# Values of four heads in one load and results of two heads in one store, in an attention kernel bound by its transfers

## The chip, the cores and the metric

The kernel runs on one core of a Trainium2 chip. The metric is device time in microseconds (us), the median of several executions. Executions of one kernel mostly agree within 0.2%. The time of a run is some 1 to 3 us more than the span that a profile shows from its first to its last instruction, so spans are compared with spans and times with times.

## The reference

```python
# scores [8, 12, 1024, 1024] fp32, v [8, 12, 1024, 64] fp32: 96 heads
attn = np.exp(scores - np.max(scores, axis=-1, keepdims=True))
attn = attn / (np.sum(attn, axis=-1, keepdims=True) + 1e-8)
return np.matmul(attn, v).astype(np.float32)
```

403 MB of scores have to come in. The values and the results are 25 MB each.

## The kernel before

A partition holds eight rows of one head. An iteration of the loop works on four heads (k = 0 to 3); there are 24 iterations. For each row block r of a head, ScalarE takes exponentials to fp16 (two rows at a time), TensorE transposes eight 128x128 blocks into PSUM (psT), VectorE evicts them (pt), and TensorE multiplies by the values. A column of ones beside the values gives the sum of the row. VectorE then normalises (reciprocal and multiplication) and SyncE issues the store.

```python
sc_bh = scores.rearrange("b h (p r) j -> (b h) p r j", p=P)
v_bh = v.rearrange("b h (p c) d -> (b h) p c d", p=P)      # 2 KB runs
out_bh = out.rearrange("b h (p r) d -> (b h) p r d", p=P)  # 2 KB runs
...
    # finish(): after the last row of each half of a head
    if g == G - 1:
        if r == G - 1:
            st["out_sb"] = take(out_bufs)
        recip = take(rc_bufs)
        nc.vector.reciprocal(out=recip[:], in_=psO[:, :, D : D + 1])
        nc.vector.tensor_tensor(
            out=st["out_sb"][:, r - G + 1 : r + 1, :], in0=psO[:, :, 0:D],
            in1=recip[:].to_broadcast([P, G, D]), op=mybir.AluOpType.mult)
    if r == R - 1:
        dma = nc.sync.dma_start(out=one(out_bh, n), in_=st["out_sb"][:])
        ...
def load(k, n, parts=(R,), **cond):
    queue(nc.sync.dma_start(out=v_bufs[k][:], in_=one(v_bh, n), **cond))
    ...                                        # then the scores of the head
def load_next(k, n0):
    if k < AHEAD - 2:                          # heads 0 and 1: within the iteration
        load(k, (n0 + (AHEAD + k)) % BH, cond=n0 < BH - AHEAD)
def load_last(n0):                             # heads 2 and 3: at its end, after the last store
    ...
def heads(n0):
    for k in range(AHEAD):
        nc.gpsimd.tensor_copy(out=vones_bufs[k][:, :, 0:D], in_=v_bufs[k][:])
        ...
```

All transfers go through one queue, in the order in which SyncE issues them. Below, "the third score load" is the load of the next iteration's head 2. It is the first one issued in `load_last`, so it stands behind the last store of the iteration.

The softmax here doesn't subtract the row's maximum and nothing guards it: scores larger than these inputs give would overflow.

Of the kernel before, what the change touches and what calls it, by code (L numbers as in the profile page):

```python
# [14 lines left out]
def kernel(  # L15
# [19 lines left out]
    LAG = 2  # L35
    AHEAD = 4



    sc_bh = scores.rearrange("b h (p r) j -> (b h) p r j", p=P)  # L40
    v_bh = v.rearrange("b h (p c) d -> (b h) p c d", p=P)
    out_bh = out.rearrange("b h (p r) d -> (b h) p r d", p=P)

# [5 lines left out]
    make_identity(nc, ident32)  # L49
    ident16 = const_pool.tile([P, P], FP16, name="ident16")  # L50
    nc.vector.tensor_copy(out=ident16[:], in_=ident32[:])  # L51


    vones_bufs = []
    for k in range(AHEAD):
        vo = const_pool.tile([P, C, M], FP16, name=f"vones{k}")
        nc.vector.memset(vo[:, :, D : D + 1], 1.0)  # L57
        vones_bufs.append(vo)
# [5 lines left out]

    s_bufs = buffers(sb_pool, AHEAD, [P, R, SK], FP32, "s_nat")
    v_bufs = buffers(sb_pool, AHEAD, [P, C, D], FP32, "v_sb")
    p_bufs = buffers(sb_pool, 8, [P, EB, SK], FP16, "p_nat")
    pt_bufs = buffers(sb_pool, 4, [P, SK], FP16, "pt")
    out_bufs = buffers(sb_pool, 4, [P, R, D], FP32, "out_sb")
    rc_bufs = buffers(sb_pool, 4, [P, G, 1], FP32, "recip")  # L70
    psT_bufs = buffers(ps_pool, 4, [P, SK], FP16, "psT")
    psO_bufs = buffers(ps_pool, 4, [P, G, M], FP32, "psO")
    turn = {}
# [20 lines left out]
    def one(bh, n):  # L94
        return bh[bass.ds(n, 1)].rearrange("o p r d -> (o p) r d")

    def finish(u):

        n, r, pt, st = u
        g = r % G  # L100
        if g == 0:
            st["psO"] = take(psO_bufs)
        psO = st["psO"]
        for c in range(C):
            nc.tensor.matmul(  # L105
                out=psO[:, g, :],
                lhsT=pt[:, c * P : (c + 1) * P],
                rhs=st["vones"][:, c, :],
                start=(c == 0),
                stop=(c == C - 1),  # L110
            )
        if g == G - 1:
            if r == G - 1:
                st["out_sb"] = take(out_bufs)
            recip = take(rc_bufs)
            nc.vector.reciprocal(out=recip[:], in_=psO[:, :, D : D + 1])  # L116
            nc.vector.tensor_tensor(  # L117
                out=st["out_sb"][:, r - G + 1 : r + 1, :],
                in0=psO[:, :, 0:D],
                in1=recip[:].to_broadcast([P, G, D]),  # L120
                op=mybir.AluOpType.mult,
            )
        if r == R - 1:
            dma = nc.sync.dma_start(out=one(out_bh, n), in_=st["out_sb"][:])  # L124
            for other in stores:
                apart(dma, other)
                apart(other, dma)
            apart(dma, dma)
            stores.append(dma)
            queue(dma)  # L130
# [8 lines left out]
    def load(k, n, parts=(R,), **cond):  # L139
        queue(nc.sync.dma_start(out=v_bufs[k][:], in_=one(v_bh, n), **cond))  # L140
        r = 0
        for rows in parts:
            queue(
                nc.sync.dma_start(  # L144
                    out=s_bufs[k][:, r : r + rows, :],
                    in_=one(sc_bh, n)[:, r : r + rows, :],
                    **cond,
                )
            )
            r += rows  # L150

    def load_next(k, n0):

# [3 lines left out]
    def load_last(n0):  # L157

        before = queued[-1:]

        def loads(parts2, parts3):
            queued[:] = before
            load(AHEAD - 2, (n0 + (2 * AHEAD - 2)) % BH, parts2)
            load(AHEAD - 1, (n0 + (2 * AHEAD - 1)) % BH, parts3)

        with tc.If(n0 < BH - 2 * AHEAD) as cmp:  # L166
            loads((R,), (R,))
        with cmp.Else():
            with tc.If(n0 < BH - AHEAD):
                loads((4, 4), (2, 2, 2, 2))  # L170

    def heads(n0):

        for k in range(AHEAD):
            nc.gpsimd.tensor_copy(out=vones_bufs[k][:, :, 0:D], in_=v_bufs[k][:])  # L175
            st = dict(vones=vones_bufs[k])
            for r in range(R):
                if r % EB == 0:
                    p_nat = take(p_bufs)
                    rows = 1 if k == AHEAD - 1 and r == R - EB else EB  # L180
                    for g in range(0, EB, rows):
                        nc.scalar.activation(  # L182
                            out=p_nat[:, g : g + rows, :],
                            in_=s_bufs[k][:, r + g : r + g + rows, :],
                            func=EXP,
# [3 lines left out]
                for c in range(C):  # L189
                    nc.tensor.transpose(  # L190
                        out=psT[:, c * P : (c + 1) * P],
                        in_=p_row[:, c, :],
                        identity=ident16[:],
                    )
                pt = take(pt_bufs)
                nc.vector.tensor_copy(out=pt[:], in_=psT[:])  # L196
                if r == R - 1:
                    load_next(k, n0)
                pending.append((n0 + k, r, pt, st))
                if len(pending) > LAG:  # L200
                    finish(pending.pop(0))
        while pending:
            finish(pending.pop(0))
        load_last(n0)

    assert BH % AHEAD == 0 and BH >= 2 * AHEAD
    for k in range(AHEAD):
        load(k, k)
    with tc.For_i(0, BH, AHEAD, iteration_sync="reg_based") as n0:
        queued.clear()  # L210
        heads(n0)
# [30 lines left out]
```

## Time and profile before

| | before |
|---|---|
| time | 1069.1 us (1068.7 to 1069.3) |
| span of the profiled run | 1066.8 us |
| transfers of an iteration | 12 (4 scores, 4 values, 4 stores) |
| period of an iteration, from the completion records | 43.90 us |
| share of the queue's packets in the span | 99.8% |
| last scores landed | 1057.20 us, 9.6 us before the end |

Each transfer leaves 16 completion records, one for each DMA engine. "Landed" means the last of the 16. The period is the mean distance of such completions over 20 iterations, with each transfer's 16 records averaged. This figure, and the others below that come from completion or packet records, are computed from the records in the trace; no view of the profile prints them. How the page reads is told in the prediction, with its lines.

### The profile page before, as it was taken

The numbers are of one execution on the slowest core, as the hardware profiler recorded it, in microseconds if no ns is written. First come the engines' busy times: TensorE is split into PE (matmuls) and PEld (weight loads), VectorE is DVE, ScalarE is ACT, GpSimd is POOL, SyncE is SP. The second block draws the span as 40 slices with busy tenths as digits, with TensorE's granted clock in tenths as the row PEclk, the third lists the DMA queues.
The fourth block names the chain that finished last, engine by engine and source line by source line (L and its number), as shares of the span: only waits on it lengthen the run. The fifth ranks groups of instructions, "written<-read, shape, count | busy, mean of one in ns | idle before, by whom it ended". The sixth has DMA issues, their size and how long they took to land.

```text
span 1066.8 us, 32321 instructions
## 1 busy us (share of the span) xinstructions
PE 762.6 (71%) x12288; PEld 722.4 (68%) x12288; DVE 609.8 (57%) x1157; ACT 736.3 (69%) x432; POOL 59.9 (6%) x102
## 2 busy tenths in 40 slices
PE   3766767677776777668686777767776777767777
PEld 3766766677776767667676767767666677767766
DVE  2655555555564655656565565655555555555556
ACT  4757676676867768577676766677766767667686
POOL 0000000000000000000000000000000000000000
PEclk9888888878888888987888798887898788888889
DMA  9999999999999999999999999999999999999996
GB/s 402 424 425 426 432 431 421 437 434 424 429 430 435 423 440 428 430 429 420 439 430 433 424 432 435 430 423 427 436 433 424 439 422 429 428 439 429 431 423 265
DMA packets 42051, 453.05 MB, mean 425 GB/s; under 512 B 4672, under 2 KB 4672, under 8 KB 29248
## 3 DMA queue, kind: packets, MB, share of 16 engines
q1 hardware_dynamic: 42048, 453.00, 99.8%
q8 instruction: 3, 0.05, 0.0%
HBM read 436.73 MB, written 25.17 MB: 433 GB/s over the span
## 4 chain that ended last, share of the span: by engine, by line
DMA 49%; PE 20%; PEld 9%; ACT 8%; DVE 7%; issue 3%; SPq 3%; DVEq 0%; ACTq 0%
DMA s_nat<-in_scores_dram 49%; PE psT L190 13%; ACT p_nat L182 8%; PE psO L105 7%; PEld L190 6%; DVE pt L196 5%; PEld L105 3%; DVE out_sb L117 2%; SPq L140 1%; SPq L124 1%; SPq L144 1%; DVE recip L116 0%; SPq L166 0%; DVEq L196 0%; ACTq L182 0%
## 5 line engine op out<-in xcount | busy, mean ns | idle before, releaser
L182 ACT ACTIVATE p_nat<-s_nat 128x2048 f16<-128x2048 f32 (+1 forms) x408 | 705.5, 1800 | 253.5 <-DMA s_nat<-in_scores_dram 130.6
L190 PE MATMUL psT<-ident,p_nat 128*128 128x128 f16 x6144 | 583.9, 254 | 257.0 <-ACT p_nat L182 256.1
L196 DVE COPY pt<-psT 128x1024 f16<-128x1024 f16 x768 | 519.2, 690 | 429.2 <-PE L190 138.2
L190 PEld LDWEIGHTS <-p_nat 128*128 128x128 f16 x6144 | 501.3, 154 | 274.9 <-ACT p_nat L182 271.1
L105 PE MATMUL psO<-vones,pt 128*128 128x65 f16 x6144 | 375.8, 205 | 41.8 <-DVE pt L196 37.5
L105 PEld LDWEIGHTS <-pt 128*128 128x128 f16 x6144 | 309.0, 107 | 64.0 <-DVE pt L196 60.3
L175 POOL CAST vones<-v_sb 128x512 f16<-128x512 f32 x96 | 59.2, 617 | 987.7 <-PE L105 443.7
L117 DVE TENSOR_TENSOR out_sb<-psO,recip 128x256 f32<-128x256 f32 x192 | 80.8, 421 | 4.2
L182 ACT ACT_TABLE_LOAD x24 | 30.8, 1283 | 69.6 <-DMA s_nat<-in_scores_dram 64.8
L116 DVE RECIPROCAL recip<-psO 128x4 f32<-128x4 f32 x192 | 33.4, 174 | 18.0 <-PE psO L105 18.0
L57 DVE MEMSET vones<- 128x8 f16 x4 | 0.2, 65 | 0.8 <-PEq L226 0.8
L51 DVE CAST ident<-ident 128x128 f16<-128x128 f32 x1 | 0.2, 228 | 0.3 <-POOL ident masks.py:199 0.3
masks.py:199 POOL TENSOR_SCALAR_AFFINE_SELECT ident<-ident 128x128 f32<-128x128 f32 x1 | 0.3, 293 | 0.1
masks.py:197 POOL MEMSET ident<- 128x128 f32 x1 | 0.2, 204 | 0.3 <-POOLq L226 0.3
L226 POOL MEMSET const-float32-0.0<- 128x1 f32 x1 | 0.1, 98 | 0.2 <-issue 0.2
L226 POOL MEMSET const-bfloat16-1.0<- 128x1 bf16 x1 | 0.1, 101 | 0.0
L226 POOL MEMSET const-uint8-127<- 128x1 uint8 x1 | 0.1, 101 | 0.0
L226 POOL MEMSET const-float32-1.0<- 128x1 f32 x1 | 0.1, 98 | 0.0
## 6 DMA issues: line engine op xcount, KB each, us to landing
s_nat<-in_scores_dram SPq DMA_DIRECT2D x96, 4096.0 KB, 27.1
v_sb<-in_v_dram SPq DMA_DIRECT2D x98, 256.0 KB, 20.6
out_dram<-out_sb SPq DMA_DIRECT2D x96, 256.0 KB, 18.0
s_nat<-in_scores_dram SPq DMA_DIRECT2D x2, 2048.0 KB, 19.9
s_nat<-in_scores_dram SPq DMA_DIRECT2D x4, 1024.0 KB, 18.7
```

The source lines that it names most:

```text
L51: nc.vector.tensor_copy(out=ident16[:], in_=ident32[:])
L105: nc.tensor.matmul(out=psO[:, g, :], lhsT=pt[:, c * P : (c + 1) * P], rhs=st["vones"][:, c, :], start=(c == 0), stop=(c == C - 1),)
L116: nc.vector.reciprocal(out=recip[:], in_=psO[:, :, D : D + 1])
L117: nc.vector.tensor_tensor(out=st["out_sb"][:, r - G + 1 : r + 1, :], in0=psO[:, :, 0:D], in1=recip[:].to_broadcast([P, G, D]), op=mybir.Al ...
L124: dma = nc.sync.dma_start(out=one(out_bh, n), in_=st["out_sb"][:])
L140: queue(nc.sync.dma_start(out=v_bufs[k][:], in_=one(v_bh, n), **cond))
L144: nc.sync.dma_start(out=s_bufs[k][:, r : r + rows, :], in_=one(sc_bh, n)[:, r : r + rows, :], **cond,)
L175: nc.gpsimd.tensor_copy(out=vones_bufs[k][:, :, 0:D], in_=v_bufs[k][:])
L182: nc.scalar.activation(out=p_nat[:, g : g + rows, :], in_=s_bufs[k][:, r + g : r + g + rows, :], func=EXP,)
L190: nc.tensor.transpose(out=psT[:, c * P : (c + 1) * P], in_=p_row[:, c, :], identity=ident16[:],)
L196: nc.vector.tensor_copy(out=pt[:], in_=psT[:])
L226: nc = _bacc.Bacc("TRN2", target_bir_lowering=False, num_devices=1)
```

## The change

The intent is to use fewer and longer DMA runs for the same bytes. One load brings the values of four heads in runs of 8 KB, 32 partitions per head. One store takes the results of two heads in runs of 4 KB, 64 partitions per head. To put rows and columns where this needs them, the exponentials are written in another order and the transposes use a permuted identity. Each result tile is filled by multiplications of 64 partitions. The values are cast at once on GpSimd and then spread over all partitions by 16 copies on VectorE.

```diff
-    v_bh = v.rearrange("b h (p c) d -> (b h) p c d", p=P)
-    out_bh = out.rearrange("b h (p r) d -> (b h) p r d", p=P)
+    v_bh = v.rearrange("b h (i t) d -> (b h i) (t d)", i=Q)
+    out_bh = out.rearrange("b h (j x) d -> (b h j) (x d)", j=W)
...
-    psO_bufs = buffers(ps_pool, 4, [P, G, M], FP32, "psO")
+    psO_bufs = buffers(ps_pool, 2, [P, R // G, 512], FP32, "psO")
...
+    def normalise(k, st, first, last):
+        ...
+        nc.vector.reciprocal(out=recip, in_=psO[:, :, :, D : D + 1])
+        h = k % T
+        for t in range(T):
+            part = slice(t * W, (t + 1) * W)
+            rows = st["out_sb"][h * W : (h + 1) * W, t, first * G : last * G, :]
+            nc.vector.tensor_tensor(...)        # 64 partitions
...
+        if k == AHEAD - 1:
+            if g == G - 1:
+                normalise(k, st, b, b + 1)      # head 3 in two halves
+        elif r == R - 1:
+            normalise(k, st, 0, R // G)         # heads 0 to 2 whole
+        if r == R - 1 and k % T == T - 1:       # one store for two heads
+            dma = nc.sync.dma_start(...)
...
+    def spread_v(k):
+        for s in range(S):
+            nc.vector.tensor_copy(
+                out=vones_bufs[k][s * Q : (s + 1) * Q, :, 0:D],
+                in_=v_half[k * Q : (k + 1) * Q, s],
+            )
...
         with tc.If(n0 < BH - 2 * AHEAD) as cmp:
             queued[:] = before
-            load(AHEAD - 2, (n0 + (2 * AHEAD - 2)) % BH, parts2)
-            load(AHEAD - 1, (n0 + (2 * AHEAD - 1)) % BH, parts3)
+            load(AHEAD - 2, (n0 + (2 * AHEAD - 2)) % BH)
+            load_v((n0 + 2 * AHEAD) % BH)
+            load(AHEAD - 1, (n0 + (2 * AHEAD - 1)) % BH)
...
-                loads((4, 4), (2, 2, 2, 2))
+                load(AHEAD - 2, BH - 2, (4, 4))
+                load(AHEAD - 1, BH - 1, (2, 2, 2, 1, 1))
```

## The prediction

> **What bounds the kernel now.** I read the page's engine totals first, then the DMA rows of its slices, then the queue table and the transfer list.
>
> ```profile
> PE 762.6 (71%) x12288; PEld 722.4 (68%) x12288; DVE 609.8 (57%) x1157; ACT 736.3 (69%) x432; POOL 59.9 (6%) x102
> DMA  9999999999999999999999999999999999999996
> GB/s 402 424 425 426 432 431 421 437 434 424 429 430 435 423 440 428 430 429 420 439 430 433 424 432 435 430 423 427 436 433 424 439 422 429 428 439 429 431 423 265
> q1 hardware_dynamic: 42048, 453.00, 99.8%
> s_nat<-in_scores_dram SPq DMA_DIRECT2D x96, 4096.0 KB, 27.1
> v_sb<-in_v_dram SPq DMA_DIRECT2D x98, 256.0 KB, 20.6
> out_dram<-out_sb SPq DMA_DIRECT2D x96, 256.0 KB, 18.0
> ```
>
> No compute engine is over 71%, while the 16 DMA engines are full in every slice but the last. A score load takes 27.1 us to land because others are queued ahead of it. The transfers are the bound, so only two things can shorten the run: fewer DMA microseconds for the same 453 MB, or a shorter stretch after the last score has landed. The waits and the end of the chain show that stretch:
>
> ```profile
> ACT p_nat L182 <- DMA s_nat<-in_scores_dram: 130.6, 28, 7.5
> SPq L124 <- DVE out_sb L117: 234.5, 50, 9.0
> ...
> 1055.84 0.69 DVE pt L196
> 1057.40 1.06 ACT p_nat L182
> 1060.27 0.64 DVE pt L196
> 1060.96 0.67 PE psO L105 x8
> 1061.65 0.19 DVE recip L116
> 1061.87 0.42 DVE out_sb L117
> ```
>
> In the body ScalarE waits for scores. At the end the last piece of scores lands at 1057.20 us (the completion records), and the exponential of its rows starts at 1057.40, a start that had waited for TensorE as well. So there the data and the compute arrive together, 9.6 us before the end of the span at 1066.8. Work added to the compute of the last heads is therefore not free.
>
> **What the Trainium skill says.** "DMA: Bandwidth & Descriptors", section "Why small descriptors are slow (HBM only)", gives each packet a fixed overhead of about 3 cycles beside its bytes. The trace agrees in kind: 2 KB packets last a median 84 ns, 8 KB ones 309, 32 KB ones 1213, which is 9 ns plus the bytes at 27.2 B/ns. The same page, "Anatomy of one DMA", puts about 2 us of fixed cost on one DMA. That does not apply to a full queue here: a 256 KB transfer lands 0.63 to 0.68 us after the one in front. "ScalarE: Activation LUTs", section "What ACT_TABLE_LOAD costs", gives 186 ns + 0.833 ns per element, so 1892 ns for 2048; the trace has 1901. "VectorE: DVE Perf Modes", section "Side-by-side: where the cycles go for N=2048 bf16", gives about 150 cycles plus the elements of one partition over the mode's rate of 1, 2 or 4 a cycle; the trace's eviction of 1024 fp16 values from PSUM (690 ns) and its multiplication of 256 fp32 values (421 ns) fit that at two and one elements a cycle of 0.96 GHz.
>
> **The DMA part, which is the aim.** Bytes don't change; counts do. An iteration of four heads issues 12 transfers now (4 scores, 4 values, 4 stores) and 7 after (4, 1, 2). There are two ways to price the difference, and they disagree.
>
> By packet durations: 12,288 value packets of 84.5 ns become 3,072 of 310; 12,288 store packets become 6,144 of some 160 (interpolated); some 1,900 completion packets of 9 ns go. That is 84.7 + 56.3 + 17.1 = 158 us over 16 engines, 9.9 us of the run.
>
> By landings: packets overlap a little (the DMA share in the windows is 1.01), so what counts is the interval between completions in a full queue. Averaged over 21 iterations a score load adds 9.68 us, a value load 0.634, a store 0.662; four of each make 43.90, which is the measured period. In the last iteration the score load is cut in pieces, so the sizes of interest are there: a 1 MB load of 8 KB runs adds 2.453, a 2 MB one 4.86. These points lie on a line of 2.407 us per MB plus 0.046 per transfer. So the new value load, just such a 1 MB transfer of 8 KB runs, costs 2.45 in place of 4 x 0.634 = 2.54, and two stores of 512 KB (by the line 1.25, and 0.02 more behind a load, as now) 2.53 in place of 2.65. The period falls by 0.09 + 0.12 = 0.21 us, to 43.69; over 24 iterations **5.0 us**. I choose this one: it prices exactly what the next transfer waits for.
>
> Does the queue stay full? In DMA time from the landing of an iteration's first score load: second score load lands at 9.7, stores at 12.2, third score load begins there. It is issued after the store of heads 2 and 3. Head 3 landed at -9.7, its compute takes some 12 us, so the issue comes near 3, about 9 us early. The out tiles fall from four to two double ones; the store of heads 0 and 1 lands near 11 to 12, and the multiplication that reuses its tile stands behind the third eviction of the next head, near 15. So neither wait bites.
>
> **The compute part.** VectorE loses nothing and gains two things. Values: the four casts an iteration on GpSimd (617 ns each) become one wide cast there and 4 x 4 copies on VectorE of 32x512 fp16, SBUF to SBUF, a quarter cycle per element: (150+128)/0.96 = 290 ns at most, perhaps 200; 384 of them make 80 to 110 us. The built order puts all 16 ahead of the iteration's first eviction, so one block of some 4 to 5 us. Normalisation: half the partitions in each instruction saves no time, so for three heads of four 0.18 + 2 x 0.69 = 1.56 us (now 2 x (0.17+0.42) = 1.19), and for the fourth 2 x (0.17 + 2 x 0.42) = 2.03. Over 24 iterations 24 x (3 x 0.37 + 0.84) = 47 us. VectorE comes to about 610 + 95 + 47 = 752 us, some 71%: on a par with TensorE, and under the transfers.
> GpSimd: 24 casts of 2048 columns at some 2.4 us by the 617 ns for 512; off the path. ScalarE: same elements, read as runs of 8 floats with gaps; I take 1.90 as now. TensorE: same counts.
> In the body all this hides: a head needs some 8.5 us in a burst (1036.5 to 1062 for three), the transfers give it 10.9. Even with the copies ahead of it, head 0 is caught up by head 2.
>
> **The end.** It hangs on the landing of head 93's scores, 1034.5 now, the last one that found TensorE idle. By then 94 value loads and 89 stores have landed (94 x 0.634 = 59.6 us of DMA time and 89 x 0.662 = 58.9); after, 24 value loads of 2.453 and 44 stores of 1.265: 58.9 and 55.7. So that landing comes 4.0 us earlier. From there the transfers need two stores, 2 x 4.86 for head 94, then three pieces of 1 MB and two of 0.5 MB for head 95: 22.1 us (now 22.75), and the last row then some 5 us to the end of its multiplication: 27.1 from that landing. By compute, three heads took 27.85 us from it (1034.45 to 1062.3); the block of copies adds about 1 (four transposed rows wait in PSUM meanwhile), the longer normalisation 0.4 to 0.8 a head, mostly hidden: 29 to 29.5. The last store of 0.5 MB lands 0.6 us later than one of 256 KB. If compute sets the end: -4.0 + 1.4 + 0.6 = -2.0, 1067.2. If data does: -4.0 - 0.75 + 0.6 = -4.15, 1065.0. I can't tell which and take the middle: **1066 us**, 0.3% faster.
>
> **Rivals.** First, the packet durations are right and the saving is 9.9 us, of which the end gives back some: 1060 to 1062. For it: the packet sum accounts for 99.8% of the span. Against it: landings of 1 MB and of 256 KB transfers side by side. Second, ScalarE becomes the bound: if the runs of 32 bytes slow the exponential, 1.90 would have to grow over 2.7 us before its 7.6 us a head pass 10.9; a growth of 10% would show only at the end, 2 to 3 us: 1068 to 1071. The 154 ns for weight loads from the strided p_nat against 107 from pt show that strides can cost; those are 2-byte elements apart by 16 bytes, here 32 bytes are together. Third, VectorE's copies wait on each other (each waits for the one before it), take 0.4 us each and, with TensorE held up, the queue still holds 9 us: no change in the body, 1 to 3 us at the end: 1068 to 1070. Fourth, a store that waits on two heads delays a load: against it the 9 us above; it would cost up to 24 times a few us, 1090 and more.
>
> **Range and chances.** The two ends give 1065.0 and 1067.2. Below them lies the full 5.0 us with an end 1 us shorter, 1063, and the packet rival, near 1061. Upwards the end can take 3 us more (second and third rivals). I give 1061 to 1070. A change of 2% is 21 us; no saving of DMA time allows it, and slower by that needs the second or fourth rival in full.
>
> **What would show it.** Right: q1's share stays at 99% or more with 24,900 packets in place of 42,048; the value load lands 2.45 us behind its predecessor, the store pair 1.25 to 1.28; the period is 43.7; VectorE about 750 us busy; the end from the last landing 9 to 12 us. Wrong: a period of 43.5 or less (the packet rival), slices with DMA under 9 (starvation), an exponential over 2.0 us, copies over 0.35 us.

## The result

The changed kernel takes 1075.1 us (1074.75 to 1075.75, four runs). The kernel before, on the same chip, takes 1069.1. The ratio is 1.0057, with a 95% interval of 1.004 to 1.0075. So the change is 0.6% slower, which is within 2% but outside the predicted range of 1061 to 1070. Ratios here are the mean time of one kernel's fast runs over that of the other's from the same rounds, so they are not quite the ratio of the quoted medians.

The page of the changed kernel, with the rows that answer to those of the prediction (engine totals, DMA row of the slices, queue table, transfer list):

```profile
PE 737.2 (69%) x12288; PEld 700.7 (65%) x12288; DVE 775.5 (72%) x1517; ACT 736.0 (69%) x432; POOL 48.1 (4%) x31
DMA  9999999999999999999999999999999999999993
q1 hardware_dynamic: 24912, 453.00, 98.8%
s_nat<-in_scores_dram SPq DMA_DIRECT2D x96, 4096.0 KB, 24.7
v_sb<-in_v_dram SPq DMA_DIRECT2D x24, 1024.0 KB, 18.2
out_dram<-out_sb SPq DMA_DIRECT2D x48, 512.0 KB, 10.6
```

The counts are as planned: 24,912 packets and seven transfers an iteration. VectorE has grown by 166 us. The DMA row looks as full as before. The 10.6 us of the stores is a median over two kinds: by the completion records, the store of heads 0 and 1 lands 26.1 us after its issue and that of heads 2 and 3 only 7.7 us, where an iteration's last store took 11.9 us before. So less work stands in the queue when the last store is issued, and this turns out to matter.

The groups of VectorE that are new (busy time, then mean ns of one), from the same page:

```profile
L120 DVE TENSOR_TENSOR out_sb<-psO,recip 64x512 f32<-64x512 f32 (+1 forms) x240 | 139.7, 582 | 7.7
L195 DVE COPY vones<-v_half 32x512 f16<-32x512 f16 x384 | 109.4, 285 | 23.2 <-POOL v_half L190 6.0
```

The waits of the changed kernel (us in total, times, longest):

```profile
ACT p_nat L230 <- DMA s_nat<-in_scores_dram: 228.7, 49, 5.9
PE psO L135 <- DVE out_sb L120: 39.1, 24, 1.8
...
SPq L149 <- DVE out_sb L120: 694.8, 47, 20.0
```

ScalarE waits longer for scores than before (228.7 against 130.6 us). TensorE has a new wait of 1.6 us in each iteration: the multiplications of rows 4 to 7 of head 3 wait for the normalisation of rows 0 to 3, because both halves are now one PSUM tile. The store holds SyncE for 694.8 us in all, where it was 234.5.

**Two differences in time.** The last scores land at 1057.09 us (before: 1057.20), so the transfers gained nothing. From there to the end of the span it takes 16.4 us (before: 9.6). The chain that ends last shows this stretch; with the last scores in at 1057.1, VectorE still has rows of the last head to evict seven microseconds later:

```profile
1064.11 0.68 DVE pt L248
...
1065.74 2.06 PE psO L135 x32
...
1067.83 0.19 DVE recip L115
...
1068.55 0.38 DVE out_sb L120
```

**Where the late end comes from.** This is VectorE's timeline at the start of the last iteration of the changed kernel (start, length, instruction, in brackets the idle time before it and what ended that):

```profile
1028.01 0.18 DVE L115 RECIPROCAL recip<-psO 128x4 f32<-128x4 f32 x1 [1.42 <-PE psO L135]
1028.23 0.88 DVE L120 TENSOR_TENSOR out_sb<-psO,recip 64x256 f32<-64x256 f32 x2
1029.69 5.04 DVE L195 COPY vones<-v_half 32x512 f16<-32x512 f16 x16 [0.58 <-PE psT L242]
1034.75 1.89 DVE L248 COPY pt<-psT 128x1024 f16<-128x1024 f16 x3
```

And the same place in the kernel before:

```profile
1024.03 0.42 DVE L117 TENSOR_TENSOR out_sb<-psO,recip 128x256 f32<-128x256 f32 x1
1027.89 0.69 DVE L196 COPY pt<-psT 128x1024 f16<-128x1024 f16 x1 [3.43 <-PE L190]
```

Before, VectorE is done with the old iteration 0.9 us after the first scores of the new one have come in (ScalarE's table load at 1023.54 marks that), and then idles 3.4 us until exponentials and transposes arrive. After, it is done 4.3 us after that mark (1024.81), and then the block of 16 copies takes 5.0 us more. So the first eviction stands 9.9 us behind the mark, where it stood 4.35. From the first eviction to the end of the last multiplication the four heads then take 34.2 us (before 34.4). The sum closes: first scores 1.27 us later, first eviction 5.59 us later from there, 0.23 us less for the four heads and 0.11 us more for the last store make 6.74 us, and the spans differ by 1073.51 - 1066.77 = 6.74.

**Where the transfers lost their gain.** The period of an iteration is 43.89 us, as before (43.90); 43.69 was predicted. Yet each kind of transfer costs what was predicted when one lands behind another: the value load 2.450 us, the store 1.261, a score load a median of 9.690. What is new is packets that last too long. If a packet counts as long when it lasts over 25 ns more than 9.2 ns plus its bytes at 27.2 B/ns, the kernel before has 15 such packets after the first 75 us (in which all kernels show some) and the changed one 263. Their excess, summed and divided by 16 engines, is 4.55 us (before 0.04). That is the missing saving. They lie 3 to 10 us behind the landing of an iteration's first scores, which is where SyncE issues the last store and the third score load.

### The profile page after: what moved, and what is told of

It reads as the page before. It is cut to its first block, busy times and chain, and to the rows that moved or that the text cites. A ratio compares the mean times of both kernels' runs of the same rounds, so it can differ in the third digit from the quotient of the medians.

```text
span 1073.5 us, 32452 instructions
## 1 busy us (share of the span) xinstructions
PE 737.2 (69%) x12288; PEld 700.7 (65%) x12288; DVE 775.5 (72%) x1517; ACT 736.0 (69%) x432; POOL 48.1 (4%) x31
## 3 DMA queue, kind: packets, MB, share of 16 engines
q1 hardware_dynamic: 24912, 453.00, 98.8%
## 4 chain that ended last, share of the span: by engine, by line
DMA 60%; PE 18%; ACT 7%; DVE 5%; issue 3%; SPq 3%; PEld 3%; DVEq 0%; ACTq 0%; PEldq 0%
DMA s_nat<-in_scores_dram 60%; PE psT L242 11%; ACT p_nat L230 7%; PE psO L135 7%; DVE out_sb L120 2%; DVE pt L248 2%; PEld L242 2%; SPq L183 1%; SPq L171 1%; PEld L135 1%; SPq L149 1%; DVE vones L195 0%; DVE recip L115 0%; SPq L209 0%; ACTq L230 0%
## 5 line engine op out<-in xcount | busy, mean ns | idle before, releaser
L230 ACT ACTIVATE p_nat<-s_nat 128x2048 f16<-128x2048 f32 (+1 forms) x408 | 705.2, 1800 | 260.1 <-DMA s_nat<-in_scores_dram 228.7
L242 PE MATMUL psT<-order,p_nat 128*128 128x128 f16 x6144 | 582.5, 249 | 141.8 <-ACT p_nat L230 137.2
L248 DVE COPY pt<-psT 128x1024 f16<-128x1024 f16 x768 | 511.4, 689 | 227.2 <-PE psO L135 94.3
L242 PEld LDWEIGHTS <-p_nat 128*128 128x128 f16 x6144 | 490.3, 153 | 152.7 <-ACT p_nat L230 150.6
L135 PE MATMUL psO<-vones,pt 128*128 128x65 f16 x6144 | 355.2, 205 | 187.9 <-DVE pt L248 147.8
L135 PEld LDWEIGHTS <-pt 128*128 128x128 f16 x6144 | 297.1, 106 | 213.4 <-DVE pt L248 166.3
L120 DVE TENSOR_TENSOR out_sb<-psO,recip 64x512 f32<-64x512 f32 (+1 forms) x240 | 139.7, 582 | 7.7
L195 DVE COPY vones<-v_half 32x512 f16<-32x512 f16 x384 | 109.4, 285 | 23.2 <-POOL v_half L190 6.0
L190 POOL CAST v_half<-v_sb 128x2048 f16<-128x2048 f32 x25 | 47.4, 1897 | 1000.6 <-DMA v_sb<-in_v_dram 704.4
L115 DVE RECIPROCAL recip<-psO 128x8 f32<-128x8 f32 (+1 forms) x120 | 22.8, 190 | 34.0 <-PE psO L135 19.8
## 6 DMA issues: line engine op xcount, KB each, us to landing
out_dram<-out_sb SPq DMA_DIRECT2D x48, 512.0 KB, 10.6
```

The costliest lines, as they stand in the source:

```text
L115: nc.vector.reciprocal(out=recip, in_=psO[:, :, :, D : D + 1])
L120: nc.vector.tensor_tensor(out=rows.rearrange("j (b g) d -> j b g d", g=G), in0=psO[part, :, :, 0:D], in1=recip[part].to_broadcast([W, last ...
L135: nc.tensor.matmul(out=st["psO"][:, b, g * M : (g + 1) * M], lhsT=pt[:, c * P : (c + 1) * P], rhs=st["vones"][:, c, 0:M], start=(c == 0), ...
L190: nc.gpsimd.tensor_copy(out=v_half[:], in_=v_sb[:])
L195: nc.vector.tensor_copy(out=vones_bufs[k][s * Q : (s + 1) * Q, :, 0:D], in_=v_half[k * Q : (k + 1) * Q, s],)
L230: nc.scalar.activation(out=p_nat[:, g : g + rows, :].rearrange("p r (s v) -> p s r v", s=S), in_=s_bufs[k][:, r + g : r + g + rows, :].rea ...
```

## The experiments

Three theories for the transfers were tried, one after the other. **P**: a burst of issues that falls late into the load in flight disturbs them, whatever made it late. **B**: large transfers straight behind each other do, above all the first two score loads, which have nothing between them any more. **Q**: the third score load is issued too late, behind the two-head store, so that the faster DMA engines run nearly out of work. For the end there was one theory (the copies and the late normalisation add up) and, as rivals, that one of the two alone does it. The texts are quoted as they stood before each run, with letters of their own: A is the block of 16 copies as the cause of both losses, C the normalisation on 64 partitions and the two-head stores, D the common PSUM tile, F an early form of P, and L (in store_pad and values_pad) the shared completion semaphores. All results were correct, but for one run that is named.

### First four: each half of the change alone, the copies elsewhere, the copies alone

store_only keeps the store part and takes the values back to the code of before. values_only is the reverse.

```diff
# store_only, against the changed kernel
+        queue(nc.sync.dma_start(out=v_bufs[k][:], in_=one(v_bh, n), **cond))
...
-            spread_v(k)
+            nc.gpsimd.tensor_copy(out=vones_bufs[k][:, :, 0:D], in_=v_bufs[k][:])
# values_only, against the changed kernel
-        if r == R - 1 and k % T == T - 1:
+        if r == R - 1:
+            dma = nc.sync.dma_start(out=one(out_bh, n), in_=st["out_sb"][:])
```

> Only the stores are changed (two heads in one 512 KB store, permuted transposes, half-partition normalisation); values as before. Theory A (the 16 value copies on VectorE, in one 5.0 us block at the start of each iteration, cause both losses): no block, so the stream gains its 2.9 us (24 x 0.12), the end grows by at most 1 to 1.5 us from the longer normalisation and the larger last store; 1066.5 to 1068.5 us, score packets over 1233 ns as few as before (65). Rival C (the normalisation on 64 partitions and the stores of two heads hold the compute up): 1072 or more. Rival B (score loads queued back to back lengthen the packets): value loads still stand between them, so few long packets.

> Only the values are changed (one 1 MB load for four heads, cast, 16 copies, permuted exponential); stores and normalisation as before. Theory A: the whole loss is here: end from the last landing some 15 us as in the changed kernel (9.6 before), and the stream loses 4 to 5 us by some 250 long packets while it gains 2.0: 1074 to 1076 us. Rival C: the loss is not here: 1067 to 1069. Rival B: the long packets stay, since loads stand back to back except for small stores, and the end is short: 1069 to 1071.

Measured: store_only 1162.2 us (ratio 1.0868, interval 1.085 to 1.0886), values_only 1153.9 us (1.0789, 1.0771 to 1.0807). Both are far slower than either whole kernel, and neither was foreseen. The waits of SyncE say why, first of store_only, then of values_only:

```profile
SPq L167 <- DMA v_sb<-in_v_dram: 218.0, 22, 10.5
SPq L171 <- DMA s_nat<-in_scores_dram: 201.1, 23, 8.9
```

```profile
SPq L156 <- DMA s_nat<-in_scores_dram: 487.0, 25, 21.9
```

SyncE waits, before it issues a load, for another load to land. The completion records show the reason: an iteration's transfers take eight completion semaphores in turn, and the turn begins anew with each iteration. A semaphore is not taken again before its last transfer has landed. With 12 transfers (before) or seven (after) this falls on transfers that have long landed, or are soon to. With nine, the ninth and the next iteration's first share a semaphore and stand side by side in the queue; with ten it is two pairs. These two runs therefore measure the number of transfers, not the parts of the change; the same two parts with 12 transfers, in the second four, take 1084.2 and 1072.5 us.

spread_pool moves the copies to GpSimd. before_copies adds 16 such copies, of no use, to the kernel before, at the same place.

```diff
# spread_pool, against the changed kernel
-            nc.vector.tensor_copy(
+            nc.gpsimd.tensor_copy(
                 out=vones_bufs[k][s * Q : (s + 1) * Q, :, 0:D],
# before_copies, against the kernel before
+        for k in range(AHEAD):
+            for q in range(4):
+                nc.vector.tensor_copy(
+                    out=idle_b[k][q * 32 : (q + 1) * 32, :, 0:D],
+                    in_=idle_a[k * 32 : (k + 1) * 32, q],
+                )
```

> The changed kernel with the 16 copies moved from VectorE to GpSimd; transfers the same. Theory A: the block is gone; the end from the last landing falls from 16.4 to 10 to 11.5 us; if the copies also caused the long packets, the last score lands near 1052.5 in place of 1057.1: 1063 to 1066 us. If the long packets come from loads queued back to back (rival B) they stay: end short, landing near 1057: 1068 to 1070. Rival C: 1073 or more.

> The kernel before with 16 idle copies of the same shape and the same quarters of partitions on VectorE at the start of each iteration, into tiles that nobody reads; transfers the same. Theory A: end from the last landing from 9.6 to 14 to 15 us (1073 to 1074), and if the copies themselves lengthen packets, the last landing 4 to 5 us later (1077 to 1079). Rival B: long packets don't come, so 1073 to 1074. Rival C: nothing much, 1069 to 1071.

Measured: spread_pool 1071.7 us (1.0026, 1.0009 to 1.0043), before_copies 1068.7 us (1.000, 0.9983 to 1.0016). Taking the copies off VectorE brings the end from 16.4 to 12.1 us behind the last landing. The landing itself stays (1057.5 us), and so do the long packets (4.39 us). So the copies cost some 4 us at the end and nothing in the stream. In the kernel before, the same block costs nothing at all:

```profile
1024.01 0.42 DVE L120 TENSOR_TENSOR out_sb<-psO,recip 128x256 f32<-128x256 f32 x1
1025.35 5.06 DVE L179 COPY idle_b<-idle_a 32x512 f16<-32x512 f16 x16 [0.91 <-DVE out_sb L120]
1030.44 1.89 DVE L205 COPY pt<-psT 128x1024 f16<-128x1024 f16 x3
```

The block begins in the 3.4 us in which VectorE idled, delays the first eviction by 2.5 us, and the four heads catch up on these, since they waited for data (31.9 us instead of 34.4). In the changed kernel the old iteration ends late, and the block then stands behind it.

### Second four: the parts again with 12 transfers, head 3 in one piece, another order

store_pad and values_pad are the two halves with tiny loads of 512 bytes added (two and three in an iteration), so that the count is 12 again. values_pad also issues the value load ahead of the third score load. no_split normalises head 3 whole, as the other heads. order_v puts the value load behind the first score load.

```diff
# store_pad, against store_only (values_pad is alike, with three)
+    def pad(j):
+        rows = v.rearrange("b h s d -> (b h s) d")
+        queue(nc.sync.dma_start(out=pad_bufs[j][:], in_=rows[0:16, 0:8]))
# no_split, against the changed kernel
-        if k == AHEAD - 1:
-            if g == G - 1:
-                normalise(k, st, b, b + 1)
-        elif r == R - 1:
+        if r == R - 1:
             normalise(k, st, 0, R // G)
# order_v, against the changed kernel
+            if k == 0:
+                load_v((n0 + 2 * AHEAD) % BH, cond=n0 < BH - 2 * AHEAD)
...
-            load_v((n0 + 2 * AHEAD) % BH)
```

> The stores alone changed, as in the first store run, with two tiny loads of 16 rows of 32 bytes an iteration so that twelve transfers share the eight completion semaphores exactly as before. Theory L (the 1162 us of the store run came from its ten transfers: loads waited for the landing of a load issued just before on the same semaphore): the queue is full again and the time falls to 1066 to 1070. If it stays over 1100, theory L is wrong. Theory D (rows 4 to 7 of an iteration's last head wait for the multiplication of rows 0 to 3, since both banks are one tile): about 2 us more at the end than before, so nearer 1068 to 1070; end from the last landing 11.5 to 12.5.

> The values alone changed, with three tiny loads an iteration for the same purpose. Theory L: full queue. The stream gains 2 us at most and keeps the long packets away if they come from score loads standing back to back (here a store stands between them): last landing near 1055, end some 9.6 us later: 1067 to 1069, for the 5 us block of copies cost nothing in the kernel before. If the long packets come with the one large value load or the permuted exponential, last landing near 1059 and 1071 to 1072.

> The changed kernel with the last head normalised whole, like the other three, in place of in halves. Theory D: the stall of TensorE before the last 32 matmuls of each iteration (39 us in all, 1.6 to 1.8 each) is gone, the multiplications after the last matmul grow from 0.9 to 1.4 us, so each iteration's compute ends 1.5 to 2 us earlier; the end from the last landing falls from 16.4 to 13 to 14.5 us: 1071.5 to 1073.5. If the stall is no cause: 1075 to 1076.

> The changed kernel with the value load issued after the first score load of the next iteration in place of between the last two, so that no three score loads stand back to back. Rival B (back to back loads lengthen packets): the 4.5 us of long packets fall under 1 us and the last landing comes at 1052 to 1054, the end follows as far as compute allows: 1071 to 1073. Rival F (the burst of issues right behind the last store of an iteration lengthens the packets in flight): three issues remain of four, long packets fall by a third at most: 1074 to 1075.

Measured: store_pad 1084.2 us (1.0142, 1.0125 to 1.0159), values_pad 1072.5 us (1.0031, 1.0014 to 1.0048), no_split 1074.0 us (1.0046, 1.0029 to 1.0063). Two numbers carry weight. First, values_pad has almost no long packets (0.05 us) and a period of 43.81: the value part saves the 0.09 us that were predicted for it. store_pad has 1.70 us of long packets and no saving (43.92). So the loss in the stream comes with the store. Second, the old iteration's last multiplication ends 1.3 us behind the mark of the new one before, 1.4 in values_pad, 3.5 in store_pad, 4.6 in the changed kernel (means over 21 iterations). So the store part makes the end late and the value part puts its copies behind it. The times of the two carry less. In store_pad's last iteration the multiplication waits once for a cast that had waited for a score load on a shared semaphore:

```profile
PE psO L139 <- POOL vones L210: 12.2, 1, 12.2
```

Without that it would be near 1072 us (an estimate: 1084.2 less 12.2). In values_pad, head 94's first exponential starts only when the second half of its scores has landed, some 5 us late. no_split shortens the delay by 0.7 us. Its time is 1.1 us lower, but the intervals of the two ratios overlap, and it misses the 1071.5 to 1073.5 us of its theory: the wait on the common PSUM tile is real but small.

order_v gave a wrong result (relative error 1.36): the value load overtook the cast of the values it replaces. Its time says nothing.

### Third four: theories P and Q, and the late end without its causes

before_late holds back the last reciprocal of each iteration of the kernel before by 14 copies (4.7 us). order_v2 is order_v repaired. banks_pool is the changed kernel with the copies on GpSimd and one PSUM tile per half head, so that neither cause of the late end is left. banks_pool_early is banks_pool with the third score load issued ahead of the iteration's last store.

```diff
# before_late, against the kernel before
+            if k == AHEAD - 1 and r == R - 1:
+                for q in range(14):
+                    after(nc.vector.tensor_copy(...))   # ahead of the reciprocal
# banks_pool, against the changed kernel
-    psO_bufs = buffers(ps_pool, 2, [P, R // G, 512], FP32, "psO")
+    psO_bufs = buffers(ps_pool, 4, [P, G, M], FP32, "psO")
...
-            nc.vector.tensor_copy(
+            nc.gpsimd.tensor_copy(
# banks_pool_early, against banks_pool
+        elif k == AHEAD - 2:
+            load(k, (n0 + (AHEAD + k)) % BH, cond=n0 < BH - 2 * AHEAD)
...
-            load(AHEAD - 2, (n0 + (2 * AHEAD - 2)) % BH)
```

> The kernel before with 14 idle copies on VectorE (4.4 us) between the last eviction of each iteration and its last reciprocal, so that the last multiplication, the last store and the burst of loads behind it come some 3.4 us later, as in the changed kernel (4.6 us behind the landing of the next head in place of 1.3). The end is 3.4 us later in any case: 1072.5. Theory P (long packets come where the burst of issues falls that late into the load in flight, whatever made it late): 3 to 5 us of long packets, last landing 1060 to 1062: 1075.5 to 1077.5. If not P: last landing 1057.

> The changed kernel with the copies on GpSimd and with one PSUM tile per bank, every head normalised by halves as before. Theory D: no stall of TensorE before the last 32 matmuls; the last multiplication 2 us nearer to the landing of the next head (4.6 to about 2.5); the end from the last landing 10 to 10.5 us (12.1 with the copies moved alone). Theory P: long packets fall from 4.4 to 1 to 2 us, last landing 1054 to 1055: 1066 to 1068. If P is wrong but D right: 1069 to 1070.

> As banks_pool, with the third score load of the next iteration issued before the last store, so that it isn't held by that store and only the store, the value load and the fourth score load stand in the burst. Theory P: long packets under 1 us, last landing 1052.5 to 1054, 1064 to 1066. If the long packets have nothing to do with the burst: as banks_pool.

> The changed kernel with the value load issued right behind the first score load of the next iteration, this time with the cast ahead of it in the program (the first try cast the values of the wrong iteration). Rival B (three score loads back to back): long packets under 1 us, last landing 1052 to 1054, 1070 to 1073. Theory P: the burst is as late as before, with three loads less one: 3 to 4.5 us of long packets stay, 1074 to 1076.

Measured: before_late 1072.9 us (1.0041, 1.0025 to 1.0058), banks_pool 1070.4 us (1.0013, 0.9996 to 1.0029), banks_pool_early 1071.0 us (1.0018, 1.0001 to 1.0034), order_v2 1088.6 us (1.0185, 1.0166 to 1.0204).

- **P fell.** In before_late the old iteration's last multiplication ends 5.3 us behind the mark of the new one, later than in the changed kernel (4.6). It pays 3.7 us for this at the end (13.3 us behind the last landing instead of 9.6), but has only 0.24 us of long packets.
- **The late end is explained for the most part.** In banks_pool the end is 11.95 us behind the last landing, within the 9 to 12 of the prediction (its own expectation, 10 to 10.5, missed), at a nearly unchanged landing of 1056.9 us. Of the 2.4 us that are left over the kernel before, 1.8 come from the landing, which follows the first scores of the last iteration sooner: after 31.9 us there, after 33.7 before. VectorE's timeline shows the block gone:

```profile
1028.40 0.88 DVE L119 TENSOR_TENSOR out_sb<-psO,recip 64x256 f32<-64x256 f32 x2
1029.75 1.29 DVE L246 COPY pt<-psT 128x1024 f16<-128x1024 f16 x2 [0.47 <-PE L240]
```

- **Q gained.** banks_pool_early moves nothing but the third score load. Its long packets fall from 4.03 to 0.90 us (0.65 of it in the last iteration) and its period to 43.69 us, although its old iterations end 6.3 us behind the mark (banks_pool: 3.9), which speaks against P once more. The time did not follow, for two reasons of this build. In the last iteration its second store comes when most engines have no work left: the issue ends at 1031.57 us, and the fastest engine was done at 1028.57. And its exponentials of head 2 wait on a semaphore shared with the value load:

```profile
ACT p_nat L229 <- DMA v_sb<-in_v_dram: 160.0, 22, 7.4
```

- **B lost.** order_v2 has the value load between the first two score loads, where the long packets lie, and more of them (11.66 us), not fewer. Its value load also has to wait for the cast of the values before it, so the run is not a clean one.

### Fourth: the third load moved, and the converse

after_early is the changed kernel with the third score load moved ahead of the last store. Two more things change with it, though its text says one: the value load now stands behind the fourth score load, and head 94's scores come as one piece where they came in two halves. (The clean move is banks_pool_early, above.) before_later is before_late with 24 copies instead of 14. banks_pool_early2 is banks_pool with the move of after_early.

```diff
# after_early, against the changed kernel
-        if k < AHEAD - 2:
+        if k < AHEAD - 1:
             load(k, (n0 + (AHEAD + k)) % BH, cond=n0 < BH - AHEAD)
...
-            load(AHEAD - 2, (n0 + (2 * AHEAD - 2)) % BH)
-            load_v((n0 + 2 * AHEAD) % BH)
             load(AHEAD - 1, (n0 + (2 * AHEAD - 1)) % BH)
+            load_v((n0 + 2 * AHEAD) % BH)
...
-                load(AHEAD - 2, BH - 2, (4, 4))
# before_later, against before_late
-                for q in range(14):
+                for q in range(24):
```

> The changed kernel with one thing moved: the third score load of an iteration is queued ahead of its last store (after head 2's exponentials) instead of behind it. Theory Q (the load held behind the two-head store runs the queue of the fastest DMA engines nearly dry): long packets in the body fall from 4.55 us to below 1 us, the last scores land at 1053 to 1054.5 us instead of 1057.1, and the time falls to 1069 to 1072 us, since the late end (16 us after the landing) is untouched. Rival (the long packets come from the large transfers themselves, wherever the load is issued): long packets stay at 4 us or more, landing at 1057, time 1075 us.

> The kernel before with 24 idle copies (about 7 us) ahead of the last reciprocal of an iteration, which holds its last store and so the third score load back some 7 us. Theory Q: the fastest DMA engines run nearly dry, so the body shows 3 us or more of long packets, the last scores land at 1060 us or later, and the time is 1078 to 1081 us. Rival (lateness of the load has nothing to do with it, the large transfers have): long packets below 0.5 us, last landing 1057 to 1058 us, time 1075.5 to 1077 us from the later end alone.

> Both repairs together: copies on GpSimd and one PSUM tile per bank (no late end), and the third score load ahead of the last store, this time with the exponentials' semaphore not shared with the value load. If the two causes are the whole of it: last scores land at 1053 to 1054.5 us, the end comes 10 to 12.5 us later, 1064 to 1067 us, which is what was predicted for the change. If the gain in the stream is given back in a third place: 1069 us or more.

Measured: after_early 1069.5 us (1.0008, 0.9993 to 1.0024), before_later 1109.9 us (1.0377, 1.0361 to 1.0393), banks_pool_early2 1069.3 us (1.0007, 0.9994 to 1.0021).

after_early's edit takes the ratio from 1.0057 to 1.0008, some 5 us. Its long packets fall from 4.55 to 0.14 us and its period to 43.68 us; the last scores land at 1052.31 us instead of 1057.09. The queue's side can be read from SyncE's timeline, here the last store of an iteration and the third score load. In the kernel before around 542 us:

```profile
541.94 0.33 SPq L124 DMA_DIRECT2D out_dram<-out_sb  x1
543.41 0.35 SPq L144 DMA_DIRECT2D s_nat<-in_scores_dram  x1
```

When this load's issue ended (543.76), the fastest engine had 7.4 us of work left (until 551.17). In the changed kernel around 547 us:

```profile
546.96 0.35 SPq L149 DMA_DIRECT2D out_dram<-out_sb  x1
547.85 0.35 SPq L171 DMA_DIRECT2D s_nat<-in_scores_dram  x1
```

By the completion records of that iteration, the first scores landed at 542.14 us. The work queued ahead of these two issues, the second score load and the store of heads 0 and 1, was completed at 549.36 us on the fastest of the 16 engines and at 553.07 on the slowest. So the fastest engine had 2.1 us of work left when the store was issued (its issue ended at 547.31), and 2.4 us, with the new store, when the score load was. In after_early:

```profile
567.08 0.36 SPq L149 DMA_DIRECT2D out_dram<-out_sb  x1
568.40 0.34 SPq L171 DMA_DIRECT2D s_nat<-in_scores_dram  x1
```

Here the load is issued at the end of head 2's exponentials, 23 us before the work ahead of it is done on the fastest engine (591.98 us). The mean over the engines doesn't tell this: that engines finish a transfer independently is stated by the Trainium skill, "DMA: Bandwidth & Descriptors", section "Why a DMA increments its semaphore by 16 and not by 1". The traces agree: the first and the last of the 16 completions of a large transfer lie 2.3 to 3.1 us apart before and 2.7 to 4.1 after. So I call **lead** the time from the end of an issue to the completion, on the fastest engine, of the transfer ahead of it. The smallest lead of all issues of an iteration, as a mean over 20 iterations, beside the long packets:

| kernel | smallest lead, us | long packets, us | period, us |
|---|---|---|---|
| before_later | 1.2 | 25.07 | 45.41 |
| order_v2 | 1.8 | 11.66 | 44.32 |
| spread_pool | 2.5 | 4.39 | 43.89 |
| changed kernel | 2.5 | 4.55 | 43.89 |
| banks_pool | 2.8 | 4.03 | 43.87 |
| no_split | 3.1 | 3.79 | 43.86 |
| before_late | 3.5 | 0.24 | 43.90 |
| store_pad | 4.3 | 1.70 | 43.92 |
| values_pad | 6.4 | 0.05 | 43.81 |
| before_copies | 7.5 | 0.04 | 43.90 |
| before | 7.6 | 0.04 | 43.90 |
| banks_pool_early | 8.3 | 0.90 | 43.69 |
| after_early | 15.2 | 0.14 | 43.68 |
| banks_pool_early2 | 15.6 | 0.26 | 43.68 |

The order is not perfect: store_pad stands out (its single leads go down to 2.8 us), and banks_pool_early does by its last iteration alone. But the two pairs that move only the time of issue, banks_pool to banks_pool_early and before_late to before_later, move the long packets in both directions. And B falls: after_early and banks_pool_early have the same large transfers, the first two score loads still back to back, and few long packets. The converse went much further than expected: before_later was to take 1078 to 1081 us under Q and took 1109.9. With a lead of 1.2 us the fastest engines run dry: by the packet records, fewer than 16 packets are in flight for 45.9 us between 75 and 1000 us, a mean of some 2 us an iteration (before: none; changed kernel: 1.7 us in all). And a late load makes the next heads late as well. The packets' share of the span tells the two costs apart:

```profile
q1 hardware_dynamic: 42048, 453.00, 98.4%
```

98.4% of 1109.1 us is 1091.4 us of packet time, 26.7 more than before (99.8% of 1066.8), nearly all of it long packets. The other 15.6 us of the longer span are time without packets, 8.1 of them at the end (17.7 us from the last landing instead of 9.6).

The end of after_early was expected and stays late, 14.5 us behind the last landing. That of banks_pool_early2 was not: 14.6 us, with neither copies nor a common tile in its way. ScalarE's timeline of that kernel shows a wait that the edit itself had brought:

```profile
1030.72 7.32 ACT L226 ACTIVATE p_nat<-s_nat 128x2048 f16<-128x2048 f32 x4 [1.06 <-DMA s_nat<-in_scores_dram]
1041.84 14.63 ACT L226 ACTIVATE p_nat<-s_nat 128x2048 f16<-128x2048 f32 x9 [3.80 <-DMA s_nat<-in_scores_dram]
```

Head 94's scores, now one piece, land at 1041.7 us. ScalarE idles 3.8 us for them, and then the exponentials of two heads fill the rest.

### Last two: both repairs

after_early3 and banks_pool_early3 bring head 2's scores in two halves again, in every iteration (eight transfers).

```diff
# both, against after_early and banks_pool_early2
+            parts = (4, 4) if k == AHEAD - 2 else (R,)
-            load(k, (n0 + (AHEAD + k)) % BH, cond=n0 < BH - AHEAD)
+            load(k, (n0 + (AHEAD + k)) % BH, parts, cond=n0 < BH - AHEAD)
```

> after_early with the load of head 2 of each iteration in two halves, so that head 94's first half lands some 5 us before its second, as in the kernels before and changed (in after_early it is one piece, and the exponentials of the last two heads, 14.6 us of them, all wait for its landing at 1041.3 us). If the whole piece is what held the end of after_early: the last exponential starts at about 1052.5 instead of 1055 us, the span falls by 1 to 2.5 us, and the time is 1067 to 1068.5 us, limited then by the copies at the start of the last iteration (34 us of work from their end). Rival (the end is set by the matmul and copy chain alone): 1069 to 1070 us as in after_early.

> The same edit on banks_pool_early2, which has neither the copies on VectorE nor the split stall. Last scores land at 1052.5 to 1053 us as there; the last exponential starts at 1053 instead of 1055.4 us, the span ends 10 to 12 us after the landing: 1064 to 1066 us, faster than the kernel before by 0.3 to 0.45%. Rival (something other than the whole piece held the end): 1069 us again.

Measured: after_early3 1069.9 us (1.0008, 0.9994 to 1.0022), banks_pool_early3 1068.5 us (0.9997, 0.9984 to 1.0011). Neither hits its expectation. In after_early3, ScalarE no longer waits for head 94 as a whole, but the end is where the other limit puts it: the copies end at 1030.25 us, and the four heads take 33.7 us from there. So the split alone gains nothing while the copies are on VectorE. In banks_pool_early3 the end is 10.5 us behind the last landing, as the prediction had it, and the mean engine delivers the last scores at 1051.35 us, only 1.05 us later than in banks_pool_early2 (1050.30). But the slowest engine delivers them 4.4 us later still, at 1055.7 us, where in banks_pool_early2 it trailed by 2.4. From 550 us on, one engine falls behind by some 0.25 us an iteration. A smaller drift of this kind is in the kernel before too (the spread between first and last engine grows from 2.3 to 3.1 us) and in after_early3 (2.2 to 3.4), so it is not the edit's own. I have one profile of each and no run that takes this apart, so its cause stays open. Had that engine trailed by 2.4 us only, the time would be near 1066.6 us (an estimate: 1068.5 less 1.9). The best version is thus level with the kernel before, not better.

## Why the prediction was wrong

**The prices of the transfers: right.** 24,912 packets (24,900), the value load 2.450 us behind its predecessor (2.45), the store 1.261 (1.25 to 1.28). In after_early the period is 43.68 us (43.69), and head 93's scores land 4.2 us earlier than before (4.0). The first rival, which priced packet durations at 9.9 us, fell: no kernel has a period near 43.5.

**The compute part: right in kind.** The copies take 285 ns (290 at most). VectorE is busy for 775 us (752 predicted, 3% under). The exponentials take a mean of 1800 ns in both kernels, so the second rival fell.

**"It is issued after the store of heads 2 and 3 ... so the issue comes near 3, about 9 us early": the first step that failed.** In the iteration shown above, the issue ended 6.1 us after the first scores had landed, not 3. The store of two heads waits for the second head's normalisation, which is late for the reasons below. And the slack was counted to the moment at which the slowest engine would have finished (12.2 us), while the fastest was through with what was queued ahead after 8.5 us. Together this left 2.4 us in place of 9. It is the fourth rival, "a store that waits on two heads delays a load", set aside on the strength of those 9 us. It cost 4.6 us in the landing of head 93's scores (0.6 us later than before, where 4.0 earlier was predicted). It did not show as predicted for starvation either: no slice but the last falls under 9, because a packet that takes longer counts as busy. after_early, which moves this load (and the value load), gives the saving back; banks_pool_early, which moves it alone, has the predicted period, 43.69 us; before_later, which delays it in the other kernel, produces the loss. Why a packet lasts longer when the queue is short, no run here shows.

**"The block of copies adds about 1" and "head 0 is caught up by head 2": the second step that failed.** The end came 16.4 us after the last landing, where the two variants of the prediction amount to 10.2 (9.6 and 0.6 for the larger store) and 12.3 (9.6, less 2.0, with the 4.75 by which the landing was to come earlier). The last four heads take 34.2 us from their first eviction. From 1035.12 us on ScalarE never waits for scores, so compute alone sets this time, and nothing is caught up: a first eviction that is 5.6 us later is an end some 5.4 us later. In before_copies, whose first eviction was late too, the four heads took 31.9 us. So their compute has become at least 2.3 us longer with the change (VectorE is busy for 27.6 us of it against 25.2, at a granted clock of 0.90 against 0.93). The step added the block to a VectorE that is free, and it counted on heads that catch up, which these don't. In the kernel before it is free for 3.4 us at that place, and there the block costs nothing (before_copies). In the changed kernel the half-partition normalisations and the wait on the common PSUM tile, 1.6 us an iteration, have already used that time up. The copies alone cost nothing at the end (before_copies, 9.4 us), the late old iteration alone leaves 12.1 us (spread_pool), and the two together make 16.4. With both taken away (banks_pool) the end is 11.95 us behind the landing. The third rival had the copies costing 1 to 3 us at the end; spread_pool measured 4.3.

**The sum.** 4.6 us of landing and 5.2 us of end (16.4 against the middle, 11.2) make 9.8, and the time was 9.1 us over the predicted 1066. (The spans of the two profiled runs differ by 6.7 us, the medians of the times by 6.0.)

## What to carry to other kernels

When a change makes one transfer wait for more work, check the issue that stands behind it in the queue: count its slack from the real end of that work to the moment when the fastest DMA engine is through with what is queued ahead, and distrust a full busy row. When a change adds two delays at one place, look up how long the engine is idle there and charge what exceeds it once, for the sum. A count of transfers per iteration that makes neighbours share a completion semaphore can cost more than the change under test, so look at the waits of the issuing engine before you believe a run with half a change undone.

## What the Trainium skill lacked or had wrong

- "DMA: Bandwidth & Descriptors" doesn't say how far ahead of a busy queue's end a transfer must be issued for nothing to be lost. Here a smallest lead of 2.5 us on the fastest engine came with 4.55 us of long packets a run, one of 1.2 us with 25 us, and leads from 6.4 us up with under 1 us.
- The same page does not say that the spread between the first and the last engine can grow over a run: it went from 2.7 to 5.4 us in banks_pool_early3, from 2.3 to 3.1 in the kernel before, and stayed at 2.8 to 2.9 in after_early.
- I found no page that says that packets can last longer than their size accounts for when the queue is nearly dry, so that the busy share hides it: the changed kernel shows nines in every slice but the last, with 4.55 us of such time.
- I found no page with the cost of transfers that take a small set of completion semaphores in turn: 9 or 10 transfers on eight semaphores made this kernel 8 to 9% slower than the kernel before with its 12.
- "VectorE: DVE Perf Modes", section "Side-by-side: where the cycles go for N=2048 bf16", held where it was used: an estimate of 290 ns at most by its rule for a copy of 32x512 fp16 values, 285 measured.
